# Layer 0 of a hybrid encoder trunk: the gate logits' product is put ahead of the small low-rank projections, its transposes between the first one's two products

## The chip, the cores and the metric

The kernel runs on 1 core of one Trainium2 chip. A core has a matrix engine (PE; its weight loads are listed as PEld), a vector engine (DVE), a scalar engine (ACT), GpSimd (POOL), and SP, which here only issues DMAs. Each engine works its own list of instructions in order and waits on semaphores for the others. The metric is the device time of one execution in microseconds, as a median over runs; a profiled execution gives a trace of every instruction.

## The reference

Two layers over 1024 tokens of width 1024. Layer 0 (even) is the one that the change touches:

```
h    = rmsnorm(x, norm_mix_g[i])
proj = h @ even_w_in[e]
dh   = token_shift(h) - h
xw = h + dh*mu_lora[0];  xa = h + dh*mu_lora[1];  xg = h + dh*mu_lora[2]
w_log = -softplus(-(w0 + tanh(xw @ w1) @ w2)) - 0.5
a = sigmoid(a0 + (xa @ a1) @ a2)
g = sigmoid(xg @ g1) @ g2
...
beta = sigmoid(beta_logit)
g    = -exp(a_log) * softplus(alpha_logit + dt_bias)
```

Group A (RWKV-7, 8 heads of 64) uses the three small projections `w1`, `a1` (64 columns each) and `g1` (128 columns). Group B (gated DeltaNet, 4 heads of 128) uses 8 logits per token, the last 8 columns of the input projection. Both groups then run a chunked recurrence, an output projection, a squared-ReLU MLP and a gated embedding; layer 1 is chunked attention with the same tail. All sums are float32.

## The kernel before

Activations lie transposed, width on 128 partitions in 8 pieces, tokens along the free axis. Layer 0 is worked in two halves of 512 tokens (`hf` 0 and 1), each half in 8 units (`u` 0 to 7 and 8 to 15): rwkv and gdn by turns, one head pair or head each.

A wide product (`dense_part`, `mm3`) is float32 by three fast matmuls on split operands: weight high part times input high part and times input low part, then weight low part times input high part, for each of 8 pieces of the width: 24 matmuls of 128x512 into one PSUM bank. Its weights are loaded into a `wraw` buffer (two of them), split by ACT into `whi` (line 316) and by DVE into `wlo` (line 317), two buffers each. PSUM has two dense banks, taken by turns (`bank`, line 197); for the first three products of the kernel three other banks are lent (`extra`). An evacuation multiplies the bank by the row norm `rs` on DVE (line 703 in `project`, line 728 in `lora`).

Work is written out by cooperating generators ("lanes", `run`, line 133): front, mid, back and post of each unit, and `l0_in`, which writes the wide products. A lane is resumed when a planned time has come that counts PE time alone, plus fixed latencies from a table; `mark` tells other lanes that something exists. The trace shows that the order on the engines is not simply the order of the text: the split of `wa` (line 634 of the text, after the first three projections) ran on DVE at 24.25 us, ahead of the row norm's chain at 27.34 us, which the text writes earlier. Within one bank the products keep their order.

At the first unit of a half (`u % 8 == 0`), `l0_in` does the following. It scales and splits the half's input into `xg`, and takes the sums of squares. In half 0 it then does the three rwkv projections of unit 0, whose evacuations are held back until the row norm is known (`late`, `plan`, lines 628 and 346): `row_stats` on PE and DVE, then four transposes that spread the norm to rows (`to_rows`, line 391; ACT copy at line 399). Then it calls `lora(0, ...)` (the decay and rate projections, key "la"): one DMA of the raw weights (line 714), two scalings on GpSimd by 1-mu and mu (line 722, both wide tiles), two splits, two wide products, and an add on GpSimd of the second, shifted by one token (line 732). Its result, through tanh and a split, is `lwa`, without which no rwkv front can go on. Then the unit is marked as in (`("in", u)`), which lets the front of unit 0 begin.

Only behind that mark come `gdn_logits` (line 735: a small DMA, a split by ACT line 741 and DVE line 742, 16 matmuls of 16x512 into a dense bank, evacuation at line 748) and `lora(1, ...)` (the gate projection, key "lg"). Between the two products of `lora(1, ...)` the call `between()` runs `gdn_scalars`: four transposes of the logits (line 755), a reduction (line 757) and some 25 small DVE and ACT instructions for beta and g, up to line 784. In half 1 (`u` = 8) `lora(0, ...)` stands ahead of the three projections of unit 8, and the logits after them.

The fronts of unit 0 put their work on DVE behind the mark: scans at line 886, then lines 894 to 940; their matrix `N` goes through DRAM (line 409) to a small-block inverse on GpSimd and back (lines 433, 435) before the mid stage can start.

Of the kernel before, what the change touches and what calls it, by code (L numbers as in the profile page):

```python
# [8 lines left out]
F32 = mybir.dt.float32  # L9
# [3 lines left out]
ALU = mybir.AluOpType  # L13
AX = mybir.AxisListType
# [3 lines left out]
P = 128  # L18
# [94 lines left out]
class Trunk:  # L113
# [466 lines left out]
    def l0_in(self, units):  # L580
        nc, a, fr = self.nc, self.a, self.fr
        self.state = {}
        self.wd, self.nw = {}, -1
        self.xg = []
        for u, (nm, p, hf) in enumerate(units):
            if u % 8 == 0:


                self.xg, squares = [], []
                if hf == 0:  # L590
                    acc = fr.tile([P, HB], F32, tag="rsbc", name="acc", bufs=2)
                    raw = self.wp.tile([P, 1024], F32, tag="wraw", name="wraw")
                    self.w_first = [self.wp.tile([P, 1024], F32R, tag=f"w{q}", name=f"w{q}") for q in ("hi", "lo")]
                    first = iter([slice(0, HB), slice(HB, T)])
                else:

                    x2 = [self.load_x(q, self.pre if q < 2 else self.wp, "ph" if q == 0 else "pl" if q == 1 else "wraw")
                          for q in range(4)]
                for k in range(NK):
                    if hf == 0:  # L600
                        if k % 2 == 0 and k < 4:
                            c = next(first)
                            nc.sync.dma_start(out=raw[:, c], in_=a["w_in"][4][:, c])
                            self.split_w(raw[:, c], HB, [z[:, c] for z in self.w_first])
                            if k == 2:
                                self.wd[4] = [self.dr.tile([P, T], F32, tag=f"wd4{q}", name="wd") for q in "hl"]
                                for d, z in zip(self.wd[4], self.w_first):
                                    nc.sync.dma_start(out=d, in_=z.bitcast(F32))
                        xr = self.t2()
                        (nc.sync if k > 1 else nc.scalar).dma_start(out=xr, in_=a["x"][k, :, 0:HB])  # L610
                    else:
                        xr = x2[k // 2][:, k % 2, :]
                    if k % 2 == 0:
                        xg2 = self.pair(k // 2)
                    xg = xg2[:, k % 2]
                    self.split_scaled(xg, xr, self.vec("mixg", k), slice(0, HB))
                    self.xg.append(xg)
                    if hf == 0:
                        squares.append(lambda k=k, xr=xr: self.square(acc, xr, k == 0))
                for f in squares:  # L620
                    f()
                sc = {}
                if hf == 0:
                    rsc = self.sm.tile([P, 4], F32, tag="rsc", name="rsc")
                    self.rs = fr.tile([P, HB], F32, tag="rsbc", name="rsbc", bufs=2)

                    self.extra = [lambda t=t: self.psm.tile([P, HB], F32, tag=t, name="dps") for t in ("y", "ch", "pm")]
                    self.late, self.plan = [], {2: lambda: self.row_stats([acc], rsc), 3: lambda: self.to_rows(rsc, self.rs)}
                    raws = yield from getattr(self, nm + "_in")(p, hf, u)
                    self.wa2 = fr.tile([P, 2, 512], F32R, tag="wa2", name="wa2")  # L630
                    wa2 = self.wp.tile([P, 512], F32, tag="wraw", name="wraw")
                    nc.sync.dma_start(out=wa2, in_=a["wa2"])
                    self.split_w(wa2, 512, [self.wa2[:, e] for e in range(2)])
                    self.g2 = self.l0.tile([P, 512], F32, tag="g2", name="g2")
                    nc.sync.dma_start(out=self.g2, in_=a["g2"])
                    self.hv = self.l0.tile([P, 2, 4], F32, tag="hv", name="hv")
                    nc.sync.dma_start(out=self.hv.rearrange("p a b -> p (a b)"),
                                      in_=a["gdnhv"].rearrange("(o c) -> o c", o=1).broadcast_to((P, 8)))
                    self.ea = self.l0.tile([P, 1, 4], F32, tag="ea", name="ea")
                    nc.scalar.activation(self.ea, self.hv[:, 0:1, :], AF.Exp)  # L640
                    acc = fr.tile([P, HB], F32, tag="rsbc", name="acc", bufs=2)
                    for q in range(4):
                        x2 = self.load_x(q, self.pre, "pl" if q % 2 else "ph")
                        for e in range(2):
                            self.square(acc, x2[:, e], q + e == 0, nc.vector)
                else:
                    self.rs = acc
                self.pst = None
                lwa = yield from self.lora(0, [(0, 64, 0), (64, 128, 1)], "la")
                nc.scalar.activation(lwa[0:64], lwa[0:64], AF.Tanh)  # L650
                sc["lwa"] = fr.tile([P, 2, HB], F32R, tag="lao", name="lao")
                self.split_scaled(sc["lwa"], lwa, None, slice(0, HB))
            if u:
                raws = yield from getattr(self, nm + "_in")(p, hf, u)
            self.state[u] = (raws, sc)
            self.mark(("in", u), 1.0)
            if u == 7:
                rsc = self.sm.tile([P, 4], F32, tag="rsc", name="rsc")
                self.row_stats([acc], rsc)
                yield "l0_in1"  # L660
                self.to_rows(rsc, acc)
            if u % 8 == 0:

                ba = yield from self.gdn_logits()
                gg = yield from self.lora(1, [(0, 128, 2)], "lg", lambda: self.gdn_scalars(hf, sc, ba))
                nc.scalar.activation(gg, gg, AF.Tanh, scale=0.5)
                nc.vector.tensor_scalar(gg, gg, 0.5, 0.5, op0=ALU.mult, op1=ALU.add)
                sc["lg"] = gg
                self.mark(("lg", hf))

        rsb = lambda: fr.tile([P, HB], F32, tag="rsbc", name="xs", bufs=2)
        pt = [self.pair(k) for k in range(2)]
        sc = [self.pair(q, F32) for q in (2, 3)]
        sc = [t[:, e] for t in sc for e in range(2)]
        yield from self.ple_proj(0, lambda k, hf: pt[k][:, hf], sc[0], lambda n: sc[1 + n % 3], rsb, self.load_w)
        yield from self.out_early(0, a["x"], self.pair, rsb, self.load_w, [("post", 7), ("post", 13), ("post", 14), ("post", 15)])
# [71 lines left out]
        nc.vector.tensor_tensor(ba[0:16, 0:HB], ps[0:16], self.rs[0:16], op=ALU.mult)  # L748
        return ba

    def gdn_scalars(self, hf, sc, ba):
        nc = self.nc
        pt = self.bank()
        for i in range(4):
            self.tr(pt[:, 16 * i:16 * i + 16], ba[0:16, i * P:(i + 1) * P], self.ident[0:16, 0:16])
        bat = self.sm.tile([P, 4, 8], F32, tag="bat", name="bat")
        nc.vector.tensor_reduce(bat, pt[:, 0:64].rearrange("p (i a c) -> p i c a", i=4, c=8), op=ALU.add, axis=AX.X)
        sh = [P, 4, 4]

        def new(nm):  # L760
# [1455 lines left out]
```

## Time and profile before

| what | value |
|---|---|
| median of 3 runs | 3000.6 us (3000.3 to 3003.67) |
| the profiled execution, device time | 2999.19 us |
| its span, first to last instruction | 2997.5 us |
| mean granted TensorE clock | 0.983 |
| PE busy | 2916.9 us (97%) |
| DVE / ACT / POOL busy | 2107.9 / 1443.0 / 470.3 us |
| layer 0 up to the last unit's stages | about 0 to 890 us of the span |

A timeline row gives start, length, engine, source line, operation, output <- inputs, shapes and count, and in brackets the idle time of that engine just before it and what ended it. Rows of a window table give the stretch, its length, the busy time of PE, PEld, DVE, ACT and POOL with their instruction counts, the granted clock (1.00 is full), and the DMA share and GB/s.

### The profile page before, as it was taken

The page shows a single profiled execution, that of the slowest core. Times are in us where ns is not written, and L with a number is a line of the kernel's source. Part 1 is how long each engine was busy: PE and PEld are TensorE (multiplying, and loading weights), DVE is VectorE, ACT ScalarE, POOL GpSimd, SP SyncE. Part 2 cuts the span into 40 slices and gives each one's busy share as a digit, 9 for nine tenths or more (in the row PEclk, how much of TensorE's full clock was granted, in tenths as well). Part 3 has the DMA queues.
Part 4 walks back from the last instruction along what each step waited for, and adds up shares of the span by engine and source line. Part 5 has one row for each costly group of instructions (what it writes and reads, how often), then busy time and mean ns, then how long its engine had stood idle before and what let it go on. Part 6 is the DMA issues. An engine that isn't in the chain of part 4 may idle for free.

```text
span 2997.5 us, 46700 instructions
## 1 busy us (share of the span) xinstructions
PE 2916.9 (97%) x17190; PEld 2423.7 (81%) x17190; DVE 2107.9 (70%) x4137; ACT 1443.0 (48%) x2828; POOL 470.3 (16%) x947
## 2 busy tenths in 40 slices
PE   7998999999999999999999899999999999999999
PEld 5776777777777888888888899999888888788887
DVE  6655674645838777787896677676859677778883
ACT  4433442323427545544443466666747554544441
POOL 5333432333400000000004211111200000000002
PEclk8999999999899999999999999999999999999999
DMA  5533323332346444664433211120366444754423
GB/s 191 205 127 123 130 92 124 110 115 79 137 138 229 167 156 143 242 197 152 153 114 113 92 45 48 44 66 24 112 223 217 147 155 151 253 179 148 147 98 118
DMA packets 205157, 412.49 MB, mean 138 GB/s; under 512 B 46352, under 2 KB 48640, under 8 KB 204928
## 3 DMA queue, kind: packets, MB, share of 16 engines
q1 hardware_dynamic: 174112, 353.40, 36.0%
q10 hardware_dynamic: 30816, 56.11, 4.9%
q8 instruction: 135, 2.21, 0.3%
q14 instruction: 94, 0.77, 0.1%
HBM read 283.54 MB, written 125.89 MB: 137 GB/s over the span
## 4 chain that ended last, share of the span: by engine, by line
PE 82%; DVE 8%; DMA 3%; ACT 3%; issue 2%; POOL 1%; SPq 0%; ACTq 0%; DVEq 0%; POOLq 0%
PE dps L180 68%; PE ch L180 2%; PE po L180 2%; PE iz L180 2%; PE pm L180 1%; PE pt L195 1%; PE sn L180 1%; PE tp L180 1%; PE py L180 1%; DVE pb L2064 1%; PE pp L180 1%; PE sf L180 1%; DVE act L1316 0%; PE sc L180 0%; DVE wlo L317 0%
## 5 line engine op out<-in xcount | busy, mean ns | idle before, releaser
L180 PE MATMUL dps<-r,act 128*128 128x512 f32 x3720 | 872.3, 392 | 1.2 <-ACT late L1433 0.8
L180 PEld LDWEIGHTS dps<-r,act 128*128 128x128 f32 x3720 | 698.2, 188 | 155.3 <-ACT late L1433 1.2
L180 PE MATMUL dps<-xg,whi 128*128 128x512 f32 x1248 | 422.8, 419 | 16.0 <-ACT whi L316 13.0
L180 PE MATMUL dps<-wq,act 128*128 128x384 f32 x1536 | 302.9, 341 | 9.1 <-DVE vs L1948 4.6
L1680 POOL TENSOR_TENSOR pn<-pn,prs 128x512 f32<-128x512 f32 x32 | 45.5, 1423 | 1540.1 <-DVE xw L1583 715.3
L180 PEld LDWEIGHTS dps<-xg,whi 128*128 128x128 f32 x1248 | 229.9, 196 | 67.0 <-ACT whi L316 14.0
L180 PEld LDWEIGHTS dps<-wq,act 128*128 128x128 f32 x1536 | 264.0, 189 | 12.2 <-DVE vs L1948 5.6
L180 PE MATMUL dps<-xg,wlo 128*128 128x512 f32 x624 | 253.4, 407 | 2.9 <-DVE wlo L317 2.9
L1315 ACT CAST act<-act 128x512 fp32r<-128x512 f32 (+2 forms) x281 | 160.1, 600 | 145.7 <-PE dps L180 70.9
L1316 DVE TENSOR_TENSOR act<-act 128x512 fp32r<-128x512 f32 (+2 forms) x281 | 181.5, 674 | 4.7 <-ACT act L1315 4.5
L1315 ACT CAST act<-late 128x512 fp32r<-128x512 f32 x210 | 123.7, 620 | 110.7 <-PE dps L180 90.4
L180 PE MATMUL dps<-act 128*128 128x512 f32 x720 | 174.9, 391 | 0.6 <-DVE late L1437 0.6
L180 PE MATMUL dps<-late,act 128*128 128x512 f32 x672 | 166.6, 392 | 0.0
L1316 DVE TENSOR_TENSOR act<-late,act 128x512 fp32r<-128x512 f32 x210 | 139.0, 687 | 38.5 <-ACT act L1315 38.3
L180 PEld LDWEIGHTS dps<-act 128*128 128x128 f32 x720 | 135.0, 188 | 30.3 <-DVE late L1437 1.0
L180 PEld LDWEIGHTS dps<-late,act 128*128 128x128 f32 x672 | 125.9, 188 | 27.7
L180 PEld LDWEIGHTS dps<-xg,wlo 128*128 128x128 f32 x624 | 121.4, 195 | 32.8 <-DVE wlo L317 5.2
L180 PE MATMUL dps<-xw,act 128*128 128x512 f32 x576 | 145.9, 392 | 0.8 <-ACT act L1315 0.8
L1583 DVE TENSOR_TENSOR xw<-xw,dps 128x512 f32<-128x512 f32 x192 | 130.3, 683 | 19.2 <-PE dps L180 19.0
L180 PEld LDWEIGHTS dps<-xw,act 128*128 128x128 f32 x576 | 107.9, 188 | 24.9 <-ACT act L1315 1.2
L2070 ACT ACTIVATE pb<-pb,mx 128x640 f32<-128x640 f32 (+4 forms) x128 | 89.2, 697 | 52.6 <-DVE mx L2064 51.6
L180 PE MATMUL po<-ptile,vs 128*128 128x256 f32 (+1 forms) x576 | 99.0, 283 | 3.8 <-ACT ptile L362 1.4
(513 smaller groups left out, 5287.8 us busy)
## 6 DMA issues: line engine op xcount, KB each, us to landing
hb<-late ACTq DMA_DIRECT2D x196, 256.0 KB
act<-hb SPq DMA_DIRECT2D x158, 256.0 KB
late<-in_w SPq DMA_DIRECT2D x60, 512.0 KB
act<-in_w SPq DMA_DIRECT2D x112, 256.0 KB
braw<-hb SPq DMA_DIRECT2D x80, 256.0 KB
wd<-whi SPq DMA_DIRECT2D x28, 512.0 KB
wd<-wlo SPq DMA_DIRECT2D x28, 512.0 KB
whi<-wd SPq DMA_DIRECT2D x28, 512.0 KB
```

What stands on the lines that cost most here:

```text
L180: return self.begin(self.nc.tensor.matmul(out, lhsT, rhs, start=start, stop=stop, skip_group_check=again))
L195: return self.begin(self.nc.tensor.transpose(out, in_, ident))
L1315: A.copy(hi, s)
L1316: V.tensor_tensor(lo, s, hi.bitcast(F32), op=ALU.subtract)
L1583: V.tensor_tensor(x[n][:, hs[hf]], x[n][:, hs[hf]], ps, op=ALU.add)
L1680: G.tensor_tensor(pn, pn, prs[:, sl], op=ALU.mult)
L2064: V.tensor_tensor_reduce(pb[:, (j0 - f0) * P:(j0 - f0 + n) * P], ps[:, 0:n * P], t, op0=ALU.add, op1=ALU.min, scale=-1.0, scalar=mx[:, 0:1 ...
L2070: A.activation(S, S, AF.Exp, bias=mx[:, 1:2] if nf else mx[:, 0:1], scale=-1.0, accum_out=l)
```

## The change

The logits' product, with its load and its split, is written ahead of `lora(0, ...)` in both halves. The four transposes and the reduction of the logits leave `gdn_scalars` and become `gdn_rows`, which runs between the two products of `lora(0, ...)`; the reduced tile `bat` is handed on in `sc`. What is left of `gdn_scalars` still runs between the two products of `lora(1, ...)`.

```diff
@@ -646,7 +646,8 @@
                 else:
                     self.rs = acc
                 self.pst = None
-                lwa = yield from self.lora(0, [(0, 64, 0), (64, 128, 1)], "la")
+                ba = yield from self.gdn_logits()
+                lwa = yield from self.lora(0, [(0, 64, 0), (64, 128, 1)], "la", lambda: self.gdn_rows(sc, ba))
                 nc.scalar.activation(lwa[0:64], lwa[0:64], AF.Tanh)
                 sc["lwa"] = fr.tile([P, 2, HB], F32R, tag="lao", name="lao")
                 self.split_scaled(sc["lwa"], lwa, None, slice(0, HB))
@@ -661,8 +662,7 @@
                 self.to_rows(rsc, acc)
             if u % 8 == 0:
 
-                ba = yield from self.gdn_logits()
-                gg = yield from self.lora(1, [(0, 128, 2)], "lg", lambda: self.gdn_scalars(hf, sc, ba))
+                gg = yield from self.lora(1, [(0, 128, 2)], "lg", lambda: self.gdn_scalars(hf, sc))
                 nc.scalar.activation(gg, gg, AF.Tanh, scale=0.5)
                 nc.vector.tensor_scalar(gg, gg, 0.5, 0.5, op0=ALU.mult, op1=ALU.add)
                 sc["lg"] = gg
@@ -748,13 +748,16 @@
         nc.vector.tensor_tensor(ba[0:16, 0:HB], ps[0:16], self.rs[0:16], op=ALU.mult)
         return ba
 
-    def gdn_scalars(self, hf, sc, ba):
-        nc = self.nc
+    def gdn_rows(self, sc, ba):
+
         pt = self.bank()
         for i in range(4):
             self.tr(pt[:, 16 * i:16 * i + 16], ba[0:16, i * P:(i + 1) * P], self.ident[0:16, 0:16])
-        bat = self.sm.tile([P, 4, 8], F32, tag="bat", name="bat")
-        nc.vector.tensor_reduce(bat, pt[:, 0:64].rearrange("p (i a c) -> p i c a", i=4, c=8), op=ALU.add, axis=AX.X)
+        bat = sc["bat"] = self.sm.tile([P, 4, 8], F32, tag="bat", name="bat")
+        self.nc.vector.tensor_reduce(bat, pt[:, 0:64].rearrange("p (i a c) -> p i c a", i=4, c=8), op=ALU.add, axis=AX.X)
+
+    def gdn_scalars(self, hf, sc):
+        nc, bat = self.nc, sc["bat"]
         sh = [P, 4, 4]
 
         def new(nm):
```

## The prediction

> **What bounds the kernel now.** I read the page's busy table and chain first, then windows over layer 0, then the PE timeline where the idle time is, and last what the waited-for engine had in its queue.
>
> ```profile
> PE 2916.9 (97%) x17190; PEld 2423.7 (81%) x17190; DVE 2107.9 (70%) x4137; ACT 1443.0 (48%) x2828; POOL 470.3 (16%) x947
> ...
> PE 82%; DVE 8%; DMA 3%; ACT 3%; issue 2%; POOL 1%; SPq 0%; ACTq 0%; DVEq 0%; POOLq 0%
> ```
>
> PE is the bound: a microsecond of PE idle time that goes, or of PE work done in idle time, can come off the end. So the question is where PE idles.
>
> ```profile
> 0.00:100.00 100.00, 78.60 (x336) 59.58 (x337) 59.55 (x114) 41.70 (x72) 50.82 (x136) 0.90 0.56 199
> 100.00:365.00 265.00, 253.18 (x2314) 195.28 (x2312) 161.70 (x375) 103.71 (x243) 93.15 (x254) 0.95 0.42 143
> 365.00:480.00 115.00, 112.40 (x1007) 87.82 (x1008) 76.09 (x205) 45.91 (x107) 42.13 (x103) 0.97 0.27 86
> ```
>
> Of some 80 us of PE idle time in the whole span, 21 lie in the first 100 us, at the lower clock of 0.90; the change's second place (365 to 480) has 2.6. The first place, closer:
>
> ```profile
> 30.74 0.65 PE L195 MATMUL st<-ident,rsc 128*128 128x128 f32 x4 [1.51 <-DVE rsc L304]
> 33.53 1.22 PE L180 MATMUL dps<-xg,whi 128*128 128x512 f32 x2 [2.14 <-ACT whi L316]
> 36.45 0.79 PE L180 MATMUL dps<-xg,wlo 128*128 128x512 f32 x1 [1.70 <-DVE wlo L317]
> ...
> 49.64 3.88 PE L180 MATMUL dps<-xg,wba 128*16 128x512 f32 x16
> 53.36 0.63 PE L180 MATMUL dps<-xg,whi 128*128 128x512 f32 x2
> ...
> 68.36 0.60 PE L195 MATMUL dps<-ident,f 16*128 16x16 f32 x4 [6.90 <-DVE f L748]
> 68.89 1.22 PE L180 MATMUL dps<-xg,whi 128*128 128x512 f32 x2
> ```
>
> Two holes. From 29.2 (30.74 less 1.51) to 36.45 PE waits three times (1.51, 2.14, 1.70) for the row norm and the first split weights of "la". At 61.4 it stops for 6.90 us: the logits' transposes wait for the logits' evacuation (L748), with the second product of "lg" and all of unit 1 behind them. The logits' product had ended at 53.5; why the evacuation came so late stands in DVE's queue:
>
> ```profile
> 61.62 1.37 DVE L886 TENSOR_TENSOR_SCAN L<-ones,f 128x128 f32<-128x128 f32 x4
> ...
> 67.03 0.69 DVE L916 SCALAR_TENSOR_TENSOR AR<-f,E 128x512 f32<-128x512 f32 x1
> 67.63 0.67 DVE L748 TENSOR_TENSOR f<-dps,rsbc 16x512 f32<-16x512 f32 x1
> ...
> 70.09 0.20 DVE L757 TENSOR_REDUCE bat<-dps 128x32 f32<-128x64 f32 x1
> ...
> 78.54 0.17 DVE L784 SCALAR_TENSOR_TENSOR gs_g<-gs_ab,ea 128x16 f32<-128x16 f32 x1
> ```
>
> It stood behind unit 0's front, which begins at the mark that the text sets before the logits. Both holes also cost clock:
>
> ```profile
> 32.00:33.50 1.50, 0.00 (x0) 0.00 (x0) 1.45 (x3) 1.48 (x3) 0.28 (x2) 0.50 0.00 0
> 33.50:36.40 2.90, 1.22 (x2) 0.50 (x2) 2.87 (x5) 0.00 (x0) 0.66 (x2) 0.50 0.20 34
> 36.40:42.00 5.60, 5.55 (x13) 4.39 (x14) 3.19 (x5) 2.77 (x5) 2.42 (x2) 0.50 0.57 181
> 42.00:53.30 11.30, 11.30 (x50) 7.76 (x50) 5.89 (x7) 4.96 (x8) 3.57 (x5) 1.00 0.41 139
> 61.40:68.30 6.90, 0.05 (x1) 0.00 (x0) 6.87 (x20) 3.04 (x6) 0.11 (x1) 0.58 0.61 228
> 68.30:73.00 4.70, 4.64 (x14) 3.79 (x15) 4.70 (x11) 0.83 (x2) 3.96 (x2) 0.52 0.01 3
> ```
>
> At 0.50 a wide matmul takes 0.43 us (5.60 by 13), at 1.00 it takes 0.226 (11.30 by 50).
>
> **The change part by part, half 0.**
>
> (a) The logits' product goes into the first hole. It needs `xg`, a dense bank (free: the first three products used lent ones), and its split weights. Its load takes the `wraw` buffer that the raw "la" weights took, so these are pushed one buffer on, to the one that the split of `wa` frees.
>
> ```profile
> 20.16 0.96 SPq L714 DMA_DIRECT2D lraw<-in_lora  x1
> ...
> 38.92 0.34 SPq L739 DMA_DIRECT2D wraw<-in_wba  x1
> ```
>
> ```profile
> 24.25 1.31 DVE L317 TENSOR_TENSOR wa<-wraw,wa 128x512 fp32r<-128x512 f32 x1 [4.49 <-ACT wa L316]
> ...
> 35.18 1.22 DVE L317 TENSOR_TENSOR wlo<-wraw,whi 128x1024 fp32r<-128x1024 f32 x1
> ...
> 40.55 1.23 DVE L317 TENSOR_TENSOR wlo<-wraw,whi 128x1024 fp32r<-128x1024 f32 x1
> ```
>
> ```profile
> 27.44 2.04 POOL L722 TENSOR_TENSOR wraw<-lraw,d_omul 128x512 f32<-128x512 f32 x2 [2.44 <-DMA lraw<-in_lora]
> ...
> 433.02 2.05 POOL L722 TENSOR_TENSOR wraw<-lraw,d_omul 128x1024 f32<-128x1024 f32 x1 [2.04 <-DMA lraw<-in_lora]
> ```
>
> ```profile
> 429.40 0.39 SPq L714 DMA_DIRECT2D lraw<-in_lora  x1
> ```
>
> The small load is issued at 20.2 instead of 38.92, the large one at 25.6 (24.25 + 1.31) instead of 20.16. The second half's load of that kind took 3.6 us (429.40 to 433.02), so it lands near 29.2 and GpSimd's scaling ends at 31.3 instead of 29.5. Nothing comes later by it:
>
> ```profile
> 31.43 0.58 ACT L399 COPY rsbc<-st 128x512 f32<-128x512 f32 x1 [7.21 <-PE st L195]
> ...
> 32.44 1.04 ACT L316 CAST whi<-wraw 128x1024 fp32r<-128x1024 f32 x1
> ...
> 49.67 1.05 ACT L316 CAST whi<-wraw 128x1024 fp32r<-128x1024 f32 x1 [2.35 <-PE dps L180]
> ```
>
> ACT reaches that split at 32.44, behind the copy of the norm: 1.1 us of cover. Without it (a load 2 us slower) the split comes 0.9 us later, still within the logits' product. That product, 16 by 0.23 = 3.7 us, then runs from 29.2 around the row norm's transposes to 33.5, and leaves the stretch 49.64 to 53.36: **-3.7**. Bounds: 0 (its split queued behind the norm on ACT and DVE, the product taking the place of what it should precede) and -3.7.
>
> (b) Clock. If PE works from 29.2 to 33.5, the remaining hole is one gap of about 2.5 us up to `wlo` at 36.4. The 13 matmuls at half rate then run at full rate: 13 by 0.20 = **-2.6**, bounds 0 and -2.6; I take the far end, since the clock fell behind 3.65 us of idling (1.51 and 2.14) in 4.3 us, more than one gap of 2.5. The Trainium skill ("TensorE: Matmul & The Clock Gate", Part 1) has the clock halved after an idle window of about 3.4 us; no single gap here was that long (1.51, 2.14, 1.70), so the trace is harsher than that reading. By the skill's rule this term is -2.6, by the harshest reading of the rows 0.
>
> (c) The transposes move between the products of "la": +0.6 there, -0.6 at 68.36. The second product of "la" now uses the bank of the first (the transposes take the other), so it waits for the evacuation at L728, 0.69 us, of which 0.6 are the transposes: **+0.3**, up to 2 if DVE is in a sum of squares. Behind it on PE stands only that product.
>
> (d) PE now ends the first product of "la" at 41.5 (36.45 + 22 by 0.23) and the second at 47.9 (0.9 for (c), 24 by 0.23), so "lg" must be ready 5.4 us earlier, at 47.9 instead of 53.36. Its scaling needs the second "la" weights split (41.8, as before, since that chain still starts from the split at 36.4), then 1.9 on GpSimd, 1.05 on ACT, 1.2 to 2.4 on DVE: 47 to 48.5. ACT no longer waits for a `whi` buffer as at 49.67, because the logits' weights no longer sit between. For this and the second "lg" weights, just in time as well, **+1.0**, bounds 0 and 4.
>
> (e) The 6.90 wait goes: between the products of "lg" PE needs nothing of the logits any more. **-6.9**, and its clock loss: 11 matmuls by 0.20 = **-2.2**. What is late next is unit 1's weights, whose loads move with the buffers they wait for. The 25 small instructions from L757 to L784 (70.09 to 78.7, other work among them) can run once `bat` exists, near 43 (41.5 and the transposes, the reduction behind them), before unit 0's front instead of amid it.
>
> Sum: -3.7 - 2.6 + 0.3 + 1.0 - 6.9 - 2.2 = **-14.1** by the end of "lg".
>
> **What reaches the end.** PE's wide work moves up by 14.
> ```profile
> 78.86 0.32 SPq L409 DMA_DIRECT2D scr<-N  x1
> ...
> 218.74 0.32 SPq L409 DMA_DIRECT2D scr<-Ng  x1
> ```
>
> ```profile
> 246.29 0.63 PE L180 MATMUL iz<-T,Ng 32*32 32x16 f32 x32 [5.47 <-ACT T L455]
> ```
>
> Unit 0's chain moves less: its matrix went out at 78.86, though AR (L916) was there at 67.7: the PE steps between stood in the order with the held "lg" product. I estimate that it goes out some 8 us earlier. The round trip through the inverse can stop PE (5.47 us at 246.29 for a matrix sent at 218.74), and units ahead of their chain meet it sooner. Between 8 and 14 I take **-10**: most of layer 0 behind 80 us is PE work back to back.
>
> **Half 1.** PE idles there for little:
>
> ```profile
> 381.89 0.73 PE L180 MATMUL dps<-xg,whi 128*128 128x512 f32 x2 [0.91 <-ACT whi L316]
> ...
> 391.61 0.49 PE L180 MATMUL ch<-Sg,KQ 128*128 128x128 f32 x2 [1.04 <-DVE Sg L1205]
> ```
>
> The logits could fill 1.9 us; against it, raw "la" weights again one buffer later and unit 8's front behind 3.7 us more PE work. I take **0**, bounds -1.9 and +4 (the 3.7 in full).
>
> So 2999.19 - 10 = 2989.2 against the profiled execution. The median of the runs is 1.4 higher; I forecast **2990**.
>
> **Rivals.**
> 1. Absorbed. PE arrives 14 us earlier but at the inverses of units 0 to 3 it waits for chains that moved by little (the 5.47 grows). For it: the chain binds there already. Against: unit 0's chain was itself held by the 6.90 wait. A gain of 4: 2996.5.
> 2. The product doesn't fill the first hole: the logits' splits stand behind the norm's copy on ACT. For it: ACT stood there for 7.21 us with other work behind. Against: `wa`'s split, written at the same place, ran at 24.25. Then terms (a) and (b) fall away and -7.8 is left, of which seven tenths arrive: 2995.
> 3. Slower: in half 1 the transposes stand between the products of "la" while DVE is busiest.
>
> ```profile
> 380.00:400.00 20.00, 18.05 (x157) 13.54 (x155) 15.94 (x35) 10.24 (x26) 6.25 (x9) 1.00 0.36 120
> ```
>
> DVE works 15.94 of 20 us there. If L748 is queued behind unit 7's front as it was behind unit 0's, PE pays 6.9 + 2.2 again, with "la" of unit 8, its three projections and its front behind, and these are late by the logits' 3.7 too: +12.8, net 2.8 above before, 3002. It decides from 10 us on. Against: other units' PE work stands around that place, so a wait of one lane need not stop PE.
>
> **How the numbers follow.** Forecast 0.60, rival 1 0.16, rival 2 0.10, rival 3 0.14. The low end is the full 14.1 and the 1.9 of half 1: 2983. The high end takes in rivals 1 and 2 and the nearer part of rival 3: 3001; the forecast's own range is 2984 to 2995. About 0.2% (6 us) is what a measurement of this kernel can tell from no change: nearly all of the forecast and half of rival 2 lie beyond it, 0.66; rival 1, the rest of 2 and a little of 3 within, 0.23; 0.11 slower.
>
> **What would show it.** Right: the 16 logits matmuls before 34 us; no wait on L748 of several us; clock 1.00 over 36 to 42 and 68 to 73; the first gate logits' reduction near 43; unit 1's projections some 14 us earlier. Wrong: the logits' matmuls behind 32.4; a new wait of PE on L728 or L748 in either half; the wait at the inverse of unit 3 longer than 5.47; unit 8's front later against the stretch around it.

## The result and the profile after

Over 8 runs each the changed kernel took 2992.43 us (2982.12 to 2996.03) against 3001.66 for the kernel before: a ratio of 0.9967, 95% interval 0.9955 to 0.998, or 9.9 us less. The profiled execution took 2989.8 us, its span is 2988.1 and its mean clock 0.987.

Half 0 first. The busy windows of the changed kernel over the stretches that were shown of before:

```profile
0.00:100.00 100.00, 88.04 (x396) 67.26 (x397) 66.07 (x125) 45.43 (x77) 55.67 (x138) 1.00 0.65 233
100.00:365.00 265.00, 256.21 (x2514) 195.19 (x2513) 169.29 (x411) 112.90 (x261) 101.89 (x263) 1.00 0.40 135
365.00:480.00 115.00, 112.80 (x963) 87.88 (x964) 59.83 (x170) 33.41 (x89) 35.61 (x97) 0.94 0.28 93
```

PE has 12.0 us of idle time in the first 100 instead of 21.4, and the granted clock is 1.00 up to 365 instead of 0.90 and 0.95. From 365 on it is 0.94 instead of 0.97. Both halves of the story are in the clock, the first number behind the five engines. The PE timeline of the changed kernel around the first place, then its DVE and its SP queue:

```profile
29.42 0.65 PE L195 MATMUL st<-ident,rsc 128*128 128x128 f32 x4
29.82 3.94 PE L180 MATMUL dps<-xg,wba 128*16 128x512 f32 x16
...
34.58 0.42 PE L195 MATMUL dps<-ident,f 16*128 16x16 f32 x4 [0.35 <-DVE f L748]
35.71 0.50 PE L180 MATMUL dps<-xg,wlo 128*128 128x512 f32 x1 [0.72 <-DVE wlo L317]
...
47.85 0.50 PE L180 MATMUL dps<-xg,wlo 128*128 128x512 f32 x1 [0.52 <-DVE wlo L317]
...
54.58 0.50 PE L180 MATMUL dps<-xg,wlo 128*128 128x512 f32 x1 [0.98 <-DVE wlo L317]
```

```profile
33.85 0.67 DVE L748 TENSOR_TENSOR f<-dps,rsbc 16x512 f32<-16x512 f32 x1
...
36.19 0.20 DVE L757 TENSOR_REDUCE bat<-dps 128x32 f32<-128x64 f32 x1
...
55.55 0.17 DVE L787 SCALAR_TENSOR_TENSOR gs_g<-gs_ab,ea 128x16 f32<-128x16 f32 x1
...
62.70 0.68 DVE L703 TENSOR_TENSOR raw<-dps,rsbc 128x512 f32<-128x512 f32 x1
```

```profile
20.47 1.03 SPq L739 DMA_DIRECT2D wraw<-in_wba  x1
25.92 0.33 SPq L714 DMA_DIRECT2D lraw<-in_lora  x1
```

The logits' product fills the hole of the row norm. Of its waits (1.51, 2.14 and 1.70) 0.35 and 0.72 are left, and the 6.90 at the logits' transposes is gone; new are 0.52 and 0.98 for the split weights of "lg". The second evacuation of "lg" (L703) stands at 62.70. Before, that row was:

```profile
77.94 0.69 DVE L703 TENSOR_TENSOR raw<-dps,rsbc 128x512 f32<-128x512 f32 x1
```

So half 0's "lg" is done 15.2 us earlier. To follow this lead, take an instruction that stands at the same place in both programs: the transposes of half 1's row norm, first of before, then of after.

```profile
374.50 0.63 PE L195 MATMUL dps<-ident,rsc 128*128 128x128 f32 x4
```

```profile
350.31 0.63 PE L195 MATMUL dps<-ident,rsc 128*128 128x128 f32 x4
```

Half 1 begins 24.2 us earlier, but the span is only 9.4 us shorter. Half 1 has given back 15 us. Windows of 20 us show where PE was slow there (changed kernel):

```profile
400.00:420.00 20.00, 19.68 (x190) 14.44 (x189) 14.49 (x36) 7.31 (x19) 3.67 (x11) 0.91 0.12 34
420.00:440.00 20.00, 18.78 (x128) 13.44 (x127) 6.68 (x14) 5.62 (x13) 12.50 (x35) 0.74 0.28 83
...
540.00:560.00 20.00, 17.52 (x170) 13.48 (x170) 4.56 (x13) 3.74 (x10) 7.09 (x25) 0.66 0.29 87
...
580.00:600.00 20.00, 18.90 (x214) 15.54 (x214) 15.93 (x50) 10.71 (x31) 5.71 (x17) 0.80 0.07 22
600.00:620.00 20.00, 20.00 (x160) 15.25 (x159) 14.04 (x31) 7.33 (x18) 10.04 (x28) 0.85 0.37 125
...
680.00:700.00 20.00, 19.22 (x139) 15.49 (x138) 8.91 (x25) 7.01 (x15) 8.66 (x31) 0.83 0.35 115
```

PE is busy for 114.1 of these 120 us, but at a clock of 0.66 to 0.91. The loss here is hardly idle time.

### The profile page after: what moved, and what is told of

Same layout as the page of the kernel before. It is cut to its first block, busy times and chain, and to the rows that moved or that the text cites. A ratio compares the mean times of both kernels' runs of the same rounds, so it can differ in the third digit from the quotient of the medians.

```text
span 2988.1 us, 46702 instructions
## 1 busy us (share of the span) xinstructions
PE 2917.3 (98%) x17190; PEld 2420.8 (81%) x17190; DVE 2100.8 (70%) x4137; ACT 1441.8 (48%) x2828; POOL 476.2 (16%) x947
## 3 DMA queue, kind: packets, MB, share of 16 engines
q8 instruction: 135, 2.21, 0.3%
## 4 chain that ended last, share of the span: by engine, by line
PE 78%; DVE 8%; DMA 6%; POOL 3%; ACT 3%; issue 2%; SPq 0%; ACTq 0%; POOLq 0%; DVEq 0%
PE dps L180 64%; PE ch L180 2%; PE po L180 2%; PE iz L180 1%; PE pt L195 1%; PE pm L180 1%; POOL subt L428 1%; POOL sub L430 1%; PE sn L180 1%; PE tp L180 1%; DVE act L1319 1%; PE py L180 1%; DMA late<-hd 1%; DMA Xp<-z 1%; PE pp L180 1%
## 5 line engine op out<-in xcount | busy, mean ns | idle before, releaser
L180 PEld LDWEIGHTS dps<-act 128*128 128x128 f32 x720 | 134.9, 188 | 31.5 <-DVE late L1440 2.3
```

What stands on the lines that cost most here:

```text
L180: return self.begin(self.nc.tensor.matmul(out, lhsT, rhs, start=start, stop=stop, skip_group_check=again))
```

## The experiments

### One half at a time

`half0` has the new order in half 0 alone, `half1` in half 1 alone. Of `half0`, against the changed kernel (`half1` has the two conditions swapped):

```diff
-                ba = yield from self.gdn_logits()
-                lwa = yield from self.lora(0, [(0, 64, 0), (64, 128, 1)], "la", lambda: self.gdn_rows(sc, ba))
+                if hf == 0:
+                    ba = yield from self.gdn_logits()
+                    lwa = yield from self.lora(0, [(0, 64, 0), (64, 128, 1)], "la", lambda: self.gdn_rows(sc, ba))
+                else:
+                    lwa = yield from self.lora(0, [(0, 64, 0), (64, 128, 1)], "la")
...
+                if hf == 1:
+                    ba = yield from self.gdn_logits()
+                gg = yield from self.lora(1, [(0, 128, 2)], "lg", lambda: self.gdn_scalars(hf, sc, ba if hf == 1 else None))
...
+    def gdn_scalars(self, hf, sc, ba=None):
+        if ba is not None:
+            self.gdn_rows(sc, ba)
```

> The new order in half 0 only; half 1 as before the change. In the changed kernel's trace the work is 15 us ahead at the end of lg, 24 us ahead when half 1's input is prepared, and only 9.7 us ahead at the end of layer 0. Theory A (half 0 is the whole gain, half 1's edit is worth nothing): 2992, like the changed kernel. Theory B (half 1's edit gave back what was lost there): 2978 to 2985, clearly below the changed kernel. Theory C (what happens between the end of lg and the end of layer 0 is a matter of where PE's gaps fall and whether the clock drops there, and differs with every order of the instructions): the time can lie anywhere from 2980 to 2998, and the lead at the end of lg is again 15 us.

> The new order in half 1 only; half 0 as before the change. Theory A: 3001, no difference from before. Theory B: 3008 to 3015, half 1's edit costs by itself. Theory C: no lead up to half 1, and then a difference of up to 8 us of either sign that comes with the clock windows of layer 0 and not with waits of the moved instructions.

Measured: `half0` 2975.75 us (2971.26 to 2980.45), ratio 0.9917 (0.9903 to 0.9931); `half1` 3011.04 us (3008.0 to 3026.19), ratio 1.0038 (1.0024 to 1.0051). The edit in half 0 is worth 24.9 us (0.0083 of 3000.3); the one in half 1 costs 11.4 by itself and 15 on top of the other (0.9967 less 0.9917). The half-0 edit alone beats both kernels. Theory B is borne out: `half1` lies in its range, and `half0` is a little below the 2978 that it named as the least.

To see what half 1 loses, I added up, for every profiled run, PE's idle time and its lost clock (busy time by one less the granted clock) over windows of about 10 us: from half 1's start (the row norm's transposes) over the next 530 us, which reaches the end of layer 0, and over the rest.

| run | half 1's start | start to end of span | PE idle, layer 0 / rest | lost clock, layer 0 / rest | what is left |
|---|---|---|---|---|---|
| before | 374.5 | 2623.0 | 15.8 / 31.5 | 20.6 / 5.1 | 2550.0 |
| half0 | 353.3 | 2620.7 | 18.5 / 30.3 | 15.9 / 4.7 | 2551.3 |
| after | 350.3 | 2637.8 | 15.5 / 34.6 | 30.6 / 4.2 | 2553.0 |
| half1 | 377.4 | 2647.1 | 19.5 / 34.1 | 34.1 / 8.1 | 2551.3 |

What is left is PE's work at full clock, the same within 3 us in these four. Between `half0` and after lie 17.1 us; 14.7 of them are clock lost in half 1's layer 0 (30.6 less 15.9), while PE idles there even 3.0 us less. What half 1 gives back is clock, not waiting, in these profiled executions, one of each kernel. (The profiled run of `half1` took 3026.19 us, 15 above its median, so its row shows more loss than its median has.)

Nearly all of the 14.7 stands in four of the windows. These are the rows of `half0`, whose half 1 begins 3 us later, for the stretches from 540 on that were shown of the changed kernel:

```profile
540.00:560.00 20.00, 20.00 (x203) 15.31 (x203) 7.58 (x23) 3.94 (x10) 11.10 (x37) 1.00 0.18 57
580.00:600.00 20.00, 19.62 (x195) 16.48 (x194) 7.16 (x22) 7.77 (x19) 11.33 (x38) 1.00 0.28 86
600.00:620.00 20.00, 19.05 (x180) 14.23 (x179) 13.36 (x33) 5.27 (x11) 4.50 (x8) 0.91 0.28 97
680.00:700.00 20.00, 20.00 (x176) 15.88 (x175) 8.72 (x29) 6.71 (x18) 8.50 (x30) 1.00 0.57 179
```

The changed kernel lost 16.0 us of clock in them (17.52 by 0.34, 18.90 by 0.20, 20.00 by 0.15, 19.22 by 0.17), `half0` 1.7. Elsewhere in this layer the two lose about the same.

### Half 0: the product's place, and the transposes' place

Both variants leave half 1 in its old order and run the transposes between the products of "lg", as before. `h0_late_tr` puts the product ahead of "la", `h0_behind` behind it, still ahead of the mark that releases unit 0's front. The lines around `lora(0, ...)` of `h0_behind`; `h0_late_tr` has the two statements the other way round:

```diff
+                lwa = yield from self.lora(0, [(0, 64, 0), (64, 128, 1)], "la")
+                if hf == 0:
+                    ba = yield from self.gdn_logits()
```

> Half 0 only: the logits' product goes ahead of la, but the four transposes and the reduction stay between the products of lg. My reasons say that the product's place is what counts, for its evacuation then stands ahead of unit 0's front on DVE: the lead at the end of lg is 14 to 15 us again and the time is that of the run with the new order in half 0, within what layer 0 scatters. The rival, that the transposes' place matters by itself (a wait on DVE for the reduction, and beta and g later), has lg end 3 us or more later.

> Half 0 only: the logits' product stays behind la, but stands ahead of the mark that lets unit 0's front begin; transposes as before. By the terms of my sum the first hole stays open (3.7 and 2.6 us not gained) and the 6.9 us wait on the logits' evacuation with its clock loss of 2.2 goes: a lead of about 8 us at the end of lg instead of 15, and some 5 us less gain at the end. The rival, that the wait of 6.9 us only moves to another instruction behind unit 0's front, has no lead at the end of lg.

Measured: `h0_late_tr` 2988.14 us, 0.9958 (0.9945 to 0.997); `h0_behind` 2994.88, 0.9987 (0.9978 to 0.9997). The lead at the end of "lg" (its second evacuation, at 77.94 before) was 15.4 and 8.8 us, as was expected of these two; in `half0` it was 13.7. The lead at half 1's start, against 374.50, was 19.2 and 9.9 us, beside 21.2 in `half0`. So getting L748 ahead of unit 0's front is worth 9.9 us there by itself (terms (e)), and putting the product into the first hole another 9.3 (terms (a) and (b)). For the transposes' place 2.0 are left, or up to 5.9: the ten profiled runs that have half 0 as in the changed kernel begin half 1 between 349.4 and 353.3.

By the ratios the three steps are 3.9, 8.7 and 12.3 us. The last one is a miss: `h0_late_tr` was expected at the time of `half0`. The transposes' place makes no difference up to the end of "lg", but it does right behind it. Windows of `half0`, then of `h0_late_tr`:

```profile
60.56:70.66 10.10, 9.79 (x50) 8.22 (x49) 9.07 (x24) 5.96 (x13) 2.95 (x5) 1.00 0.63 233
70.66:80.75 10.09, 10.09 (x57) 8.14 (x56) 7.78 (x12) 4.25 (x11) 4.93 (x4) 1.00 0.62 228
```

```profile
59.21:69.08 9.87, 4.72 (x26) 3.08 (x25) 9.73 (x20) 4.20 (x10) 5.50 (x5) 0.68 0.43 161
69.08:78.95 9.87, 9.87 (x36) 7.90 (x37) 3.96 (x19) 2.65 (x9) 1.64 (x6) 0.63 0.20 60
```

In `h0_late_tr` PE waits there for results of unit 0's front (2.21, 1.33 and 1.62 us) and loses 5.2 us of clock. DVE has the small instructions for beta and g among that front: the last of them runs at 73.42, in `half0` at 57.10. That they cause the waits is read from the order and not tested. The rest of the 12.3 us falls behind half 1's start (2627.0 us from there to the end of the span against 2620.7).

### How much does a mere shift of order do?

`mark06`, `mark10` and `mark34` are `half0` with the planned release of unit 8's front put off by 0.6, 1.0 and 3.4 us of planned time (1.6, 2.0 and 4.4 in the line below). Of the logits nothing is edited; only the order in which the lanes write their stages shifts.

```diff
-            self.mark(("in", u), 1.0)
+            self.mark(("in", u), 1.6 if u == 8 else 1.0)
```

> The new order in half 0 only, and for unit 8 the planned time at which its front may begin is 0.6 us later. No product and no transfer is moved by hand; the planner's order of the instructions in half 1 changes (some 1200 lines of the list of PE's instructions). If the order by itself, at equal work, moves the time by several microseconds, this run lies anywhere between 2968 and 2992; if only the logits' place counts, it is at 2976, within 3 us.

> As the run with 0.6 us, with 1.0 us: another order. Same two readings: anywhere from 2968 to 2992, or 2976 within 3 us.

> The new order in half 0 only, and unit 8's front planned 3.4 us later, the planned length of the logits' product. Theory F: what half 1's edit costs is that unit 8's front, and everything that follows from it, comes later against the wide products; then this run, which has that delay and nothing else of half 1's edit, loses 10 to 17 us and lies at 2986 to 2993. If the cost lies in the product's or the transposes' own place, it stays at 2976 within 3 us. If it is order scatter, it lies anywhere between and the runs with 0.6 and 1.0 us scatter as widely.

Measured: 2978.75 us, 0.9927 (0.9907 to 0.9946); 2982.22, 0.993 (0.991 to 0.995); 2982.56, 0.994 (0.992 to 0.996). Start to end of span: 2617.1, 2620.2 and 2630.2. The largest shift cost 7 us by the ratio, about half of what half 1 gives back, and its median lies below the 2986 that theory F named as the least. But the intervals of all three ratios overlap that of `half0`, and that of the largest reaches to a cost of 13 us. So a shift of unit 8's front alone is not shown to be what half 1 pays for, nor excluded as a part of it, and these runs don't show how much a mere change of order does.

### One collision in half 1

In the changed kernel's half 1 unit 9's matrix is sent to DRAM right behind two weight loads and read back 5.0 us later, and PE then waits for that inverse. The SP queue of after, then its PE:

```profile
514.21 0.32 SPq L832 DMA_DIRECT2D whi<-wd  x1
514.62 0.38 SPq L832 DMA_DIRECT2D wlo<-wd  x1
515.06 0.42 SPq L409 DMA_DIRECT2D scr<-Ng  x1
520.04 1.38 SPq L413 DMA_DIRECT2D subb<-scr  x4
```

```profile
542.51 0.30 PE L180 MATMUL iz<-T,Ng 32*32 32x16 f32 x12 [2.48 <-ACT T L455]
```

In `half0` the same store was issued 4 us behind the last load (509.94) and was read back after 2.0 us:

```profile
513.98 0.32 SPq L409 DMA_DIRECT2D scr<-Ng  x1
516.02 1.38 SPq L413 DMA_DIRECT2D subb<-scr  x4
```

`after_u9b` is the changed kernel with this one store on ACT's queue. (`after_u9` was meant to do the same, but chose the queue by a unit number that isn't 9 where the store is written. Every engine's list of instructions stayed as it was, so it is a second measurement of the changed kernel.)

```diff
-    def inverse_start(self, B, G):
+    def inverse_start(self, B, G, eng=None):
...
-        nc.sync.dma_start(out=scr, in_=B)
+        (eng or nc.sync).dma_start(out=scr, in_=B)
...
-        X = self.inverse_start(NTl, 4)
+        X = self.inverse_start(NTl, 4, nc.scalar if u == 9 else None)
```

> The changed kernel, with one DMA moved: the store of unit 9's matrix to DRAM goes through ACT's queue instead of SP's; every other instruction keeps its order. In the changed kernel that store is issued right behind two weight loads (514.21, 514.62, store at 515.06) and is read back 5.0 us later, where the run with the new order in half 0 alone has 2.0 us; PE then stops 2.48 us for unit 9's inverse and runs at half clock from about 545 to 557. Theory D (this one collision is what half 1's edit costs): the store is read back after 2 to 3 us, the 2.48 us wait and the low clock behind it go, and the time falls from 2992 to 2983 to 2987, some 6 to 9 us. Theory E (the collision is only one of many places, the loss is spread over half 1): the wait goes and the time stays within 3 us of 2992. If the transfers share the 16 DMA engines whatever the queue, the store is not faster and nothing changes.

> The changed kernel with one DMA moved: unit 9's matrix is stored by ACT's queue instead of SP's (the edit of after_u9, which had left every list of instructions as it was, done so that it takes effect). All other instructions keep their order. Theory D (half 1's loss comes from the store standing behind two 512 KB weight loads, which delays unit 9's inverse and makes PE wait and lose clock over 542 to 560): the store is read back after about 2 us instead of 5.0, PE's wait of about 2.5 us near 543 goes, the clock there is 1.00, ratio to the kernel before about 0.0955 + 0.9 = 0.9950 or less (2986 against 3001). Theory E (the loss comes from many places): the wait near 543 may go, the time stays within 3 us of the changed kernel's, ratio 0.9965 to 0.9975.

Measured: `after_u9` 2993.73 us, 0.9975 (0.9962 to 0.9988); `after_u9b` 2992.57, 0.9966 (0.9954 to 0.9978). The store on ACT's queue, and its reading back, in `after_u9b`:

```profile
518.28 0.35 ACTq L409 DMA_DIRECT2D scr<-Ng  x1
...
523.60 1.38 SPq L413 DMA_DIRECT2D subb<-scr  x4
```

It still takes 5.3 us, and the wait stays (2.51 us). The two loads are issued in the same moment (517.87 and 518.28), so the delay is that of sharing the transfers, not of the place in a queue. The Trainium skill ("DMA: Bandwidth & Descriptors", section "Issuing engines are not separate DMA queues") says just this: DMAs of different issuing engines run on the same DMA engines and interleave; the 5.3 us agree. The experiment missed its aim, since the wait was not removed. What the collision costs can be read off if nothing further behind it follows from it: at most 2.5 us of waiting and 6 of clock over 540 to 560 (17.52 by 0.34), half of the loss. It recurs: over 25 us around this place the clock lost is 5.8 to 6.1 us in all four profiled runs that have half 1 as in the changed kernel (after, `after_u9`, `after_u9b`, `half1`).

### Half 1: which part of the edit costs

Three kernels with half 0 as in the changed kernel. `h1_late_tr`: half 1's product ahead of "la", its transposes between the products of "lg". `h1_behind`: the product behind "la" but ahead of unit 8's three projections. `la_late`: the logits in their old place, but unit 8's projections ahead of "la". The line of `h1_late_tr` for "la":

```diff
-  lwa = yield from self.lora(0, [(0, 64, 0), (64, 128, 1)], "la", lambda: self.gdn_rows(sc, ba))
+  lwa = yield from self.lora(0, [(0, 64, 0), (64, 128, 1)], "la", (lambda: self.gdn_rows(sc, ba)) if hf == 0 else None)
```

and in the branch of half 1 of `h1_behind`, then of `la_late`:

```diff
   lwa = yield from self.lora(0, [(0, 64, 0), (64, 128, 1)], "la")
+  ba = yield from self.gdn_logits()
```

```diff
+  raws = yield from getattr(self, nm + "_in")(p, hf, u)
   lwa = yield from self.lora(0, [(0, 64, 0), (64, 128, 1)], "la")
...
-  if u:
+  if u % 8:
```

> Half 0 as in the changed kernel; half 1 with the logits' product ahead of la (as changed), but its transposes and reduction between lg's products (as before). If the product's place, with its load ahead of la's and 3.7 us of PE work ahead of unit 8's front, costs what half 1 gives back: as the changed kernel, ratio 0.995 to 0.998, and over 2634 us from half 1's start to the end of the span. If it is the transposes and the reduction between la's products (rival 3 in its milder form): as half0, ratio 0.990 to 0.993, under 2624 us.

> Half 0 as in the changed kernel; half 1 with the logits' product behind la, but ahead of unit 8's three projections (before: behind them), its transposes between lg's products as before. The load of la's raw weights is then first again, and PE has 3.7 us more ahead of unit 8's front, as in the changed kernel. If the loads' order at half 1's start is what costs: as half0, ratio 0.990 to 0.993, under 2624 us from half 1's start to the end. If the 3.7 us of PE work ahead of unit 8's projections and front, and the order of stages and DMAs that follows from it, is what costs: as the changed kernel, ratio 0.995 to 0.998, over 2634 us. In between: both, or neither.

> Half 0 as in the changed kernel, the logits of half 1 in their old place; only the order of half 1's wide products differs from half0: unit 8's three projections go ahead of la (as half 0 always has it) instead of behind it. No logits are moved by it. From half 1's start to the split of la's result (tile lao) it took 29.5 us in half0, 35.2 in h1_behind, 36.9 in h1_late_tr, 40.7 in the changed kernel, 46.8 in half1; here I expect 42 to 48. Theory L (what half 1 gives back comes from la's result being late for unit 8's front, whatever delays it): as the changed kernel or worse, ratio 0.995 to 0.999, 2634 us or more from half 1's start to the end. Rival P (the logits' product itself ahead of la, its load and the order that follows from it, is what costs; a late la is absorbed): as half0, ratio 0.990 to 0.993, under 2626 us.

Measured, with the time from half 1's start to the split of the result of "la" (tile `lao`, line 362) in the profiled run:

| run | median, us | ratio (95%) | "la" ready after | start to end | lost clock, layer 0 / rest |
|---|---|---|---|---|---|
| half0 | 2975.75 | 0.9917 (0.9903 to 0.9931) | 29.5 | 2620.7 | 15.9 / 4.7 |
| h1_behind | 2977.1 | 0.9914 (0.9898 to 0.993) | 35.2 | 2628.5 | 23.9 / 5.6 |
| h1_late_tr | 2991.16 | 0.9958 (0.9942 to 0.9973) | 36.9 | 2639.0 | 26.0 / 10.6 |
| after | 2992.43 | 0.9967 (0.9955 to 0.998) | 40.7 | 2637.8 | 30.6 / 4.2 |
| la_late | 2988.38 | 0.9955 (0.9939 to 0.9971) | 63.7 | 2632.1 | 18.8 / 5.3 |

`h1_behind` costs nothing that its median shows: 3.7 us more PE work ahead of unit 8's projections and front is absorbed. (Its profiled run, 4 us above the median, has 7.8 us more than that of `half0` from half 1's start on, between the two bounds that were set.) `h1_late_tr` costs 12 us (0.9958 less 0.9917), so the transposes and the reduction between the products of "la" are not the main cause: the medians of `h1_late_tr` and after differ by 1 us, the ratios by 3. What costs is the place of the product, with its load, ahead of "la". Its loss stands elsewhere than in the changed kernel: `h1_late_tr` loses no clock within 25 us around the collision's place (536.5 to 561.5), and 10.7 us between 401.5 and 436.5 (`half0` 4.7 in the same stretch of its half). So the collision is not needed for the loss.

`la_late` delays "la" without moving the logits (its projections come earlier instead), by more than the 42 to 48 us that were expected, and costs 11 us: this order loses too. But a late "la" isn't shown to be the reason. The loss doesn't grow with the delay (63.7 us late costs no more than 36.9). In the kernel before, "la" was ready 36.4 us after half 1's start, as late as in `h1_late_tr`, and the rest took 2623.0. And the profiled `la_late` lies between the two bounds that were set for its stretch (2632.1, against under 2626 and 2634 or more), with hardly more clock lost than `half0`: of its 11.4 us more, 3.5 are clock, 2.4 idle time, and 5.5 neither. So the path by which the product's place costs stays open.

## Why the prediction was right in its total, and where it wasn't

The 2990 forecast and the 2992.43 measured agree by luck, because two errors of opposite sign nearly cancel: half 0 brought 24.9 us where 10 stood, half 1 took 15 where 0 stood.

**The holes of half 0, terms (a) to (e): right.** The logits' 16 matmuls run at 29.82, the raw weights of "la" are issued at 25.92 (25.6 in the working), the wait on L748 is 0.35, the clock is 1.00. The first split weights of "lg" are complete at 47.85, within the forecast 47 to 48.5, and PE waits for them and the second ones 0.16, 0.52 and 0.98, 1.7 for a term of 1.0. The end of "lg" moved by 15.2 for 14.1, and the first projection of unit 1 is evacuated at 71.88 instead of 86.39. One detail was off: the transposes did not wait for the end of the first product of "la" but slipped into it at 34.58, so the reduction came at 36.19, not near 43. Three figures of the working don't come out as written, without changing the forecast: the terms of (d) (41.8, 1.9, 1.05, 1.2 to 2.4) add up to 46.0 to 47.2, not 47 to 48.5; 2989.2 and 1.4 are 2990.6; and the forecast's 0.60 and half of rival 2 are 0.65 at most, not 0.66. What (e) named last, the small instructions running before unit 0's front instead of amid it, got no price in the sum; `h0_late_tr`, where they run amid it, is 12.3 us slower than `half0`.

**"Between 8 and 14 I take -10": mis-sized, 24.9.** The step took it that unit 0's chain moves less than PE's wide work and that PE then meets the inverses sooner. The first half of that is true, and more so than estimated: unit 0's matrix goes out at 77.00 instead of 78.86, 1.9 us earlier, not 8. But nothing followed from it. Units 1 and 3 send theirs 9.0 and 21.0 us earlier; the rows of after:

```profile
77.00 0.32 SPq L409 DMA_DIRECT2D scr<-N  x1
...
119.16 0.32 SPq L409 DMA_DIRECT2D scr<-Ng  x1
...
197.74 0.32 SPq L409 DMA_DIRECT2D scr<-Ng  x1
```

and those of before for units 1 and 3 stood at 128.14 and 218.74. Rival 1 had the 5.47 us at unit 3's inverse grow; it is gone. PE comes for that inverse 13.1 us earlier, for a matrix sent 21.0 us earlier:

```profile
233.17 0.44 PE L180 MATMUL iz<-T,Ng 32*32 32x16 f32 x32
```

And the clock that was lost around it came back. Windows of before, then of after:

```profile
140.00:180.00 40.00, 38.43 (x376) 28.82 (x375) 24.53 (x51) 17.05 (x45) 25.31 (x68) 0.96 0.40 138
180.00:220.00 40.00, 37.82 (x415) 28.91 (x414) 21.71 (x58) 12.75 (x27) 5.84 (x15) 0.87 0.29 97
220.00:260.00 40.00, 33.32 (x236) 26.60 (x238) 21.28 (x46) 14.00 (x28) 17.00 (x41) 0.87 0.40 142
```

```profile
140.00:180.00 40.00, 38.81 (x355) 28.91 (x354) 24.61 (x57) 19.72 (x50) 19.85 (x56) 1.00 0.43 141
180.00:220.00 40.00, 37.49 (x401) 29.09 (x400) 24.73 (x62) 13.88 (x31) 16.06 (x41) 1.00 0.29 99
220.00:260.00 40.00, 38.40 (x366) 28.94 (x365) 17.65 (x44) 13.48 (x34) 9.27 (x30) 1.00 0.41 142
```

In these 120 us PE idled 10.4 us before and 5.3 after, and lost 10.8 us of clock before (38.43 by 0.04, 37.82 and 33.32 by 0.13) and none after. The lead grew from 15.2 to 24.2 by half 1's start. Added up from the span's start to there, PE idled 12.5 us less than before and lost 15.1 us less clock, and it had done 3.4 us more work. The working let a lead only shrink behind the edit; here the stages behind it were themselves losing time, and a shift could help them as well as hurt.

**"Half 1. I take 0, bounds -1.9 and +4": wrong, +11 alone and +15 here.** The bound counted the product's own 3.7 us, as if the only price of PE work at an earlier place were its length. `h1_behind` shows that those 3.7 us by themselves cost nothing that can be told from scatter; the place ahead of "la" does. Rival 3 had nearly the right size (12.8) by another mechanism: PE waiting on L748 and on the transposes. There is no such wait; the row of after in half 1 carries no bracket:

```profile
374.44 0.42 PE L195 MATMUL dps<-ident,f 16*128 16x16 f32 x4
```

and with the transposes back in their old place (`h1_late_tr`) the loss stays. Of the signs named in advance as "wrong", one came true: unit 8's front later against the stretch around it, "la" ready 40.7 us after the half's start instead of 36.4 before (29.5 in `half0`).

**What stays open** is how a product 53 us earlier (3.3 us after the half's start in after, 56.3 in `half0`), and a "la" some us later, turn into 15 us of lost clock further on in layer 0. The place that I tried carries at most half of it and could not be taken away by itself. The place around 600 isn't even the same in every execution: over 25 us there the changed kernel loses 6.5 us of clock, `after_u9` 1.7 and `after_u9b` 6.5. The order that the planner writes from half 1's start on is different throughout, and over the 530 us the clock lost lies between 12.8 (`mark06`) and 35.9 us (`after_u9b`, which has the changed kernel's order but for one store).

## What to carry to other kernels

Try an edit that stands in a loop over halves or layers in each of them alone: here one half's gain of 25 us and the other's loss of 11 to 15 were in one diff, and the sum looked like a forecast come true. Where PE is 97% busy, add up its lost clock beside its idle time from the windows; the idle time of the two orders of half 1 was the same within 1.3 us, and the difference lay in the clock. A lead that one edit makes is not a constant: follow an instruction that both programs share, at several places.

## What the runs showed of the hardware that I had not expected

The granted clock fell to one half where the profile shows hardly any PE idle time. In the changed kernel, from 408.9 to 414.5 PE runs only products of 2 to 128 columns; the windows around the end of that stretch:

```profile
409.00:412.00 3.00, 2.89 (x33) 2.27 (x33) 3.00 (x6) 1.03 (x3) 0.62 (x2) 1.00 0.02 5
412.00:415.00 3.00, 2.79 (x52) 1.96 (x53) 3.00 (x9) 0.19 (x1) 0.20 (x1) 0.94 0.00 0
415.00:418.00 3.00, 3.00 (x19) 2.12 (x17) 2.18 (x6) 1.26 (x3) 1.14 (x5) 0.50 0.44 138
```

PE idled 0.32 us in 6 and was then granted 0.50. The Trainium skill ("TensorE: Matmul & The Clock Gate", Part 1) ties the half rate to an idle window of about 3.4 us; no idle time like that is here, and the trace would fit something closer to how much the small products use the array. That is a reading of this stretch, not shown by an experiment, and the profile models the ends of matmuls, so that a busy PE may hold short gaps. If it holds, the place of a wide product among small ones matters beyond its length.

Executions of one program scatter by 14 to 20 us, the shorter ones at the higher mean clock: the changed kernel's order gave 2982 (clock 0.988) to 2996 us (0.984) in one set of runs, and 2985 (0.988) to 3005 (0.983) in another.
